# A decoder layer on one core: the late modulation sums move from VectorE to ScalarE products and accumulating DMAs

## The chip, the cores and the metric

The kernel runs on one core of one Trainium2 chip. Its time is the device time in microseconds (us) of that core for one execution of the whole program; three executions of the kernel before are known, and one execution was taken with a profile. TensorE is called PE here, its weight loads PEld, VectorE is DVE, ScalarE is ACT, GpSimd is POOL and SyncE is SP, as in the profile.

## The reference, cut to what matters

One layer, 512 tokens of width 1024, all in float32. A vector c gives six modulation vectors of width 1024 through one 1024 x 6144 matrix: shift, scale and gate of the attention half, and shift, scale and gate of the MLP half.

```python
c_act = silu(c)
mod = c_act @ w_ada + b_ada
sh1, sc1, g1, sh2, sc2, g2 = split(mod, 6)
h = rmsnorm(x, n0) * (1 + sc1) + sh1
y = token_mixer(h)                  # 8 MoBA heads, 8 sliding-window heads, output projection
x = x + g1 * rmsnorm(y, n1)
h = rmsnorm(x, n2) * (1 + sc2) + sh2
y = square(relu(h @ w1 + b1)) @ w2 + b2
x = x + g2 * rmsnorm(y, n3)
```

sh1 and sc1 are needed first and have code of their own, which the change leaves alone. The **later modulations** are g1, then sh2 and sc2 (in two halves), then g2: four units of work, each a 1024 x 1024 matrix times c_act.

## The kernel before

**The stages.** A first stage (up to about 70 us) loads x, normalises it and projects q and k for three pairs of heads. From there to about 240 us runs the attention: 64 blocks (16 heads of 4 query blocks of 128 tokens), and between their steps PE is given the rest of the input projection and, later, the output projection as filler. From about 260 us on, the MLP: 32 column groups up, 32 down, on PE almost without a gap. Each float32 matrix product is three fp32r matmuls (`mm3`, L95), for which weights and activations are split into a high and a low part: ACT makes the high part (L83), POOL or DVE the low part (L85).

**One attention block.** PE makes the scores; DVE adds the bias and takes the row extreme (L649); ACT takes the exponentials and their sum (L656); DVE takes the reciprocal (L662); POOL scales the row by it (L663, called the normalise below); PE transposes the result (L672); ACT and DVE split it (L686, L687). After the four blocks of a head PE makes its output, ACT and DVE bring it out of PSUM (L709, L710), and after each second head POOL splits it into `oth` and `otl` (L713, L715), which the output projection reads. Blocks are called w0_0 (head 0, block 0) to w15_3 below; the 64 normalises stand on POOL in this order.

**What sets the order.** PE's order is written by hand. For the other engines the library that builds the program orders each engine's instructions, within marks (`issue_after`) that put work behind the last bias on DVE and the last exponential on ACT (`anchor`, `behind`). Each engine runs its own list strictly in order, and an instruction that waits for a semaphore holds up all that stand behind it. SP issues nearly all loads, in order too.

**The late units.** `ada_wide(r, ...)` (L265) is a generator. For unit r it loads eight slices `adar{r}_0` to `adar{r}_7` of 128 x 1024 (512 KB each, four buffers, L274), and sums slice times c_act into `adaacc`, one half of 512 columns per step, by DVE (L282 for the first slice, L284 for the others): 16 steps. Then the sum over partitions is PE's: a product with ones (`adarow`, L299) for the gates, transposes (`adaps`, L242) and a DVE reduction for shift and scale. `side_at(k)` (L795) advances units 0, 1 and 2 by block number k. Unit 3 is advanced in the MLP, one step for each column group from the eighth on (L1042).

Of the kernel before, what the change touches and what calls it, by code (L numbers as in the profile page):

```python
# [23 lines left out]
AF = mybir.ActivationFunctionType  # L24
ALU = mybir.AluOpType
# [5 lines left out]
KC = DM // P  # L31
# [15 lines left out]
def layer_kernel(ctx, tc, x, c_col, ada_c, ada_r, bada_col, bada_row, gain_col, gain_row, w_in0, w_in1, w_in2,  # L47
                 w_out, w1, b1_col, w2, b2_row, rel, sinks, onehot, out):
    nc = tc.nc
# [149 lines left out]
    c_act = const.tile([P, KC], F32, name="c_act")  # L199
# [16 lines left out]
    def halves(t):  # L216
        return [t[:, 0:512], t[:, 512:1024]]
# [46 lines left out]

    def ada_wide(r, pool, then):  # L265

        acc = pool.tile([P, 1024], F32, tag="adaacc", name=f"adaacc{r}", bufs=1)
        raws = []

        def load():  # L270
            j = len(raws)
            if j < KC:
                raws.append(pool.tile([P, 1024], F32, tag="araw", name=f"adar{r}_{j}", bufs=4))
                nc.sync.dma_start(out=raws[j], in_=ada_r[r][:, j * 1024:(j + 1) * 1024])  # L274

        for _ in range(3):
            load()
        for j in range(KC):
            load()
            for a, w in zip(halves(acc), halves(raws[j])):  # L280
                if j == 0:
                    nc.vector.tensor_scalar_mul(a, w, c_act[:, j:j + 1])  # L282
                else:
                    nc.vector.scalar_tensor_tensor(a, w, c_act[:, j:j + 1], a, op0=ALU.mult, op1=ALU.add)  # L284
                yield
        then(acc)

    def gate_row(layer, g_bc, pool, tag):
# [116 lines left out]
    acc = next(g)  # L405
# [5 lines left out]
    for kc in range(KC):  # L411
# [3 lines left out]
        for k in range(18):  # L415
            if kc % 2 and nxt < KC:
                if k == 2:
                    grp = list(groups[(nxt + 2) // 2])
                    sums = ada_sums(0, grp, acc)
                    if nxt + 2 < KC:  # L420
                        g = acc0((nxt + 4) // 2)
                        acc = next(g)
# [11 lines left out]
            w, h = (w0[kc][0], hh) if k < 6 else (w0[kc][1], hh) if k < 12 else (w0[kc][0], hl)  # L434
# [37 lines left out]
    @contextmanager  # L472
    def behind():
        with ExitStack() as st:
            for ins in anchor.values():
                st.enter_context(tc.issue_after(ins))
            yield
# [308 lines left out]
    def side_steps():  # L786
        yield from ada_wide(0, wts, gate_row(0, g_bc, apool, "gt"))
        for r in range(2):
            kcs = list(range(4 * r, 4 * r + 4))
            yield from ada_wide(1 + r, wts, lambda acc: ada_cols(1, kcs, ada_sums(1, kcs, acc)))  # L790

    side = side_steps()
    sided = [1]

    def side_at(k):  # L795
        while sided[0] < 4 + min(k, 24) + max(0, min(k, 62) - 24) * 0.7 + max(0, k - 62):
            sided[0] += 1
            with behind() if k < len(blocks) else ExitStack():
                next(side, None)
# [25 lines left out]
    for k in range(len(blocks) + 8):  # L825
# [43 lines left out]
        if k < len(blocks) and blocks[k][2] == 2:  # L869
            strip_of(blocks[k][0] * 2 + blocks[k][1] + 1)  # L870
        side_at(k)
        if k < len(blocks):
            with behind():
# [158 lines left out]
    nc.sync.dma_start(out=b2_bc, in_=b2_row.to_broadcast([P, DM]))  # L1032
    g2_bc = mlp.tile([P, DM], F32, name="g2_bc")
    gate = ada_wide(3, wts, gate_row(1, g2_bc, res, "hf"))
    for f in range(3, NF):
        if f < 5:
            ws.make("both")
        w = ws.get(0 if f < 4 else 1)
# [20 lines left out]
    for f in range(NF - LAST):  # L1059
        w = ws.get()  # L1060
# [106 lines left out]
```

## Time and profile before

| | |
|---|---|
| median of three executions | 622.37 us (621.87 to 622.49) |
| the profiled execution | 623.07 us |
| its span, first to last instruction | 621.3 us, so 1.8 us lie outside it |
| PE busy | 580.3 us, 93% |
| DVE, ACT, POOL busy | 315.2, 279.2, 321.6 us |
| mean granted PE clock | 0.983 of full speed |

Busy times are sums of instructions, so a busy engine need not be the one that others wait for; what a stage waits for is read from the waits and from the order of time in that stage.

### The profile page before, as it was taken

Reading aid. Unit: us, or ns where it says so; the run is one execution under the profiler, and the core shown is the slowest. Engines: PE = TensorE matmul, PEld = TensorE weight load, DVE = VectorE, ACT = ScalarE, POOL = GpSimd, SP = SyncE. Lnnn points to the kernel's source line nnn. Section 1 sums busy time; section 2 is a strip of 40 time slices with the busy share of each in tenths; the row PEclk is TensorE's granted clock in tenths of the full one; section 3 lists DMA queues with packets and bytes.
Section 4 is the critical chain, followed back from the end, with each engine's and each line's share of the span. In section 5 each row is a group of like instructions: output and inputs, shape, how many; then the busy total and the mean of one; then the engine's idle time right before and its main releaser. Section 6 shows DMA issues by size and latency. Waiting matters only on the chain.

```text
span 621.3 us, 8137 instructions
## 1 busy us (share of the span) xinstructions
PE 580.3 (93%) x2829; PEld 482.0 (78%) x2829; DVE 315.2 (51%) x599; ACT 279.2 (45%) x532; POOL 321.6 (52%) x333
## 2 busy tenths in 40 slices
PE   2789989999897999999999999999999999999994
PEld 0477889887675888898888888788888888888883
DVE  4646679999998756535255555522401111111037
ACT  4624776578667545773233332233522333323122
POOL 1514234666898653636555555655544444446432
PEclk9969999999998999999999999999999999999998
DMA  8990569686466207734244432223232233333105
GB/s 308 419 383 1 189 129 260 128 170 224 140 185 207 84 1 270 236 106 149 89 136 136 146 125 99 80 93 101 71 112 89 100 103 102 102 101 116 56 17 186
DMA packets 29677, 89.31 MB, mean 144 GB/s; under 512 B 3427, under 2 KB 7587, under 8 KB 29636
## 3 DMA queue, kind: packets, MB, share of 16 engines
q1 hardware_dynamic: 28816, 86.52, 43.5%
q10 hardware_dynamic: 692, 2.23, 0.9%
q8 instruction: 22, 0.36, 0.3%
q14 instruction: 19, 0.16, 0.1%
q0 software_dynamic: 128, 0.05, 0.1%
HBM read 84.56 MB, written 4.22 MB: 143 GB/s over the span
## 4 chain that ended last, share of the span: by engine, by line
PE 55%; DVE 2%; ACT 2%; DMA 1%; issue 1%; POOL 0%; DVEq 0%; POOLq 0%; ACTq 0%; SPq 0%
PE u L97 9%; PE u L98 9%; PE u L96 9%; PE y L98 9%; PE y L97 9%; PE y L96 9%; DVE zg L1090 1%; ACT hf L379 1%; DMA x<-in_x 1%; ACT h2h L378 0%; DVE x L933 0%; DMA out_x<-zg 0%; ACT sq L208 0%; PE adarow L299 0%; POOL zg L1087 0%
## 5 line engine op out<-in xcount | busy, mean ns | idle before, releaser
L85 POOL TENSOR_TENSOR wlo<-raw,whi 128x512 fp32r<-128x512 f32 (+1 forms) x140 | 192.4, 1393 | 157.7 <-ACT whi L83 157.2
L83 ACT ACTIVATE whi<-raw 128x1024 fp32r<-128x1024 f32 (+5 forms) x87 | 80.7, 934 | 130.8 <-PE u L97 108.9
L97 PE MATMUL u<-h2l,whi 128*128 128x512 f32 (+1 forms) x280 | 104.2, 372 | 1.2 <-POOL h2l L380 1.1
L96 PE MATMUL u<-h2h,whi 128*128 128x512 f32 (+1 forms) x280 | 104.7, 374 | 0.0
L98 PE MATMUL u<-h2h,wlo 128*128 128x512 f32 (+1 forms) x280 | 103.8, 371 | 0.0
L97 PE MATMUL y<-wlo,ring_h2h 128*128 128x512 f32 x232 | 90.2, 389 | 0.0
L98 PE MATMUL y<-whi,ring_h2l 128*128 128x512 f32 x232 | 90.2, 389 | 0.0
L96 PE MATMUL y<-whi,ring_h2h 128*128 128x512 f32 x232 | 90.1, 389 | 0.0
L284 DVE SCALAR_TENSOR_TENSOR adaacc<-adar,c_act,adaacc 128x512 f32<-128x512 f32 x56 | 66.7, 1191 | 0.0
L97 PEld LDWEIGHTS u<-h2l,whi 128*128 128x128 f32 x280 | 52.7, 188 | 11.3 <-POOL h2l L380 1.7
L96 PEld LDWEIGHTS u<-h2h,whi 128*128 128x128 f32 x280 | 52.7, 188 | 9.2 <-ACT whi L83 0.2
L98 PEld LDWEIGHTS u<-h2h,wlo 128*128 128x128 f32 x280 | 52.7, 188 | 9.2
L663 POOL TENSOR_SCALAR w<-w,st 128x128 f32<-128x128 f32 (+2 forms) x64 | 38.2, 599 | 38.2 <-DVE st L662 32.8
L97 PEld LDWEIGHTS y<-wlo,ring_h2h 128*128 128x128 f32 x232 | 43.5, 188 | 9.1
L96 PEld LDWEIGHTS y<-whi,ring_h2h 128*128 128x128 f32 x232 | 43.5, 188 | 9.0
L98 PEld LDWEIGHTS y<-whi,ring_h2l 128*128 128x128 f32 x232 | 43.5, 188 | 9.0
L656 ACT ACTIVATE w<-w,st 128x128 f32<-128x128 f32 (+3 forms) x64 | 33.4, 522 | 28.2 <-DVE st L649 26.1
L85 POOL TENSOR_TENSOR w0lo<-w0raw,w0hi 128x384 fp32r<-128x384 f32 x16 | 17.2, 1095 | 29.3 <-ACT w0hi L83 29.3
L672 PE MATMUL p<-ident,w 128*128 128x128 f32 x136 | 25.9, 279 | 6.4 <-POOL w L663 5.9
L672 PEld LDWEIGHTS p<-ident,w 128*128 128x128 f32 x136 | 17.3, 142 | 13.4 <-POOL w L663 9.6
L686 ACT ACTIVATE pth<-p 128x384 fp32r<-128x384 f32 (+3 forms) x48 | 22.2, 466 | 10.1 <-PE p L672 9.6
L687 DVE TENSOR_TENSOR ptl<-p,pth 128x384 fp32r<-128x384 f32 (+3 forms) x48 | 25.0, 523 | 0.8 <-ACT pth L686 0.6
(222 smaller groups left out, 1093.9 us busy)
## 6 DMA issues: line engine op xcount, KB each, us to landing
raw<-in_w SPq DMA_DIRECT2D x63, 512.0 KB, 3.3
adar<-in_ada_r SPq DMA_DIRECT2D x32, 512.0 KB, 4.1
ada<-in_ada_c SPq DMA_DIRECT2D x16, 512.0 KB, 8.6
woraw<-in_w_out SPq DMA_DIRECT2D x8, 512.0 KB, 4.4
raw<-in_w_in SPq DMA_DIRECT2D x7, 512.0 KB, 6.7
w0raw<-in_w_in SPq DMA_DIRECT2D x8, 384.0 KB, 9.1
strip<-vec SPq DMA_DIRECT2D x24, 128.0 KB, 4.1
xn<-in_x SPq DMA_DIRECT2D x4, 512.0 KB, 10.0
```

The lines of the kernel that those rows point to most:

```text
L83: nc.scalar.activation(hi[:, a:b], src[:, a:b], AF.Copy)
L85: return eng.tensor_sub(lo[:, a:b], src[:, a:b], f32(hi[:, a:b])).ins
L96: nc.tensor.matmul(ps, lh, rh, start=start, stop=False, **kw)
L97: nc.tensor.matmul(ps, lh, rl, start=False, stop=False, **kw)
L98: nc.tensor.matmul(ps, ll, rh, start=False, stop=stop, **kw)
L284: nc.vector.scalar_tensor_tensor(a, w, c_act[:, j:j + 1], a, op0=ALU.mult, op1=ALU.add)
L379: nc.scalar.activation(hf[:, :n], tp, AF.Identity, bias=sh_col, scale=a_col)
L656: anchor["act"] = nc.scalar.activation(w[:, :m], w[:, :m], AF.Exp, bias=st[:, 0:1], scale=-1.0, accum_out=st[:, 1:2]).ins
L663: nc.gpsimd.tensor_scalar(w[:, :n], w[:, :n], st[:, 2:3], 1.0, op0=ALU.mult, op1=ALU.mult)
L672: nc.tensor.transpose(p_ps[:, (c0 + j) * P:(c0 + j + 1) * P], self.w[i][:, j * P:(j + 1) * P], ident)
L686: nc.scalar.activation(dst(self.pth), src, AF.Copy)
L687: nc.vector.tensor_sub(dst(self.ptl), src, f32(dst(self.pth)))
```

## The change

Each half slice is multiplied by ACT instead of DVE: slice 0 into `adaacc`, slices 1 to 7 in place in their own buffers. Slices 1 to 7 are then added onto `adaacc` by seven DMAs of 128 x 1024 with an add, issued from POOL's queue, both ends in SBUF. A unit now takes 19 steps instead of 16, and `side_at` advances faster.

```diff
@@ ada_wide @@
             for a, w in zip(halves(acc), halves(raws[j])):
-                if j == 0:
-                    nc.vector.tensor_scalar_mul(a, w, c_act[:, j:j + 1])
-                else:
-                    nc.vector.scalar_tensor_tensor(a, w, c_act[:, j:j + 1], a, op0=ALU.mult, op1=ALU.add)
+                nc.scalar.activation(w if j else a, w, AF.Copy, scale=c_act[:, j:j + 1])
                 yield
+                if j > 1 and a.offset == acc.offset:
+                    nc.gpsimd.dma_start(out=acc, in_=raws[j - 1], accum_op=ALU.add)
+        yield
+        nc.gpsimd.dma_start(out=acc, in_=raws[KC - 1], accum_op=ALU.add)
+        yield
+        yield
         then(acc)
@@ side_at @@
-        while sided[0] < 4 + min(k, 24) + max(0, min(k, 62) - 24) * 0.7 + max(0, k - 62):
+        while sided[0] < 4 + min(k, 24) * 1.2 + max(0, min(k, 62) - 24) * 0.8 + max(0, k - 62):
```

In the program that results, lines behind L284 stand four lines further down (the normalise is L667, `oth` L717, `otl` L719, the small power for the root of a norm stays L213); DVE loses 64 instructions, ACT gains 64 and POOL's queue 28 DMAs. They are called accumulates below, 0_1 to 3_7 by unit and slice.

POOL in the attention's first heads, before (w is a block's row of weights, the number behind it the head, then the block):

```order
L663 TENSOR_SCALAR w1_0_813<-w1_0_813,st1_0_864 128x128 [waits DVE_49]
L663 TENSOR_SCALAR w1_1_859<-w1_1_859,st1_1_892 128x256 [waits DVE_49,PE_49]
L663 TENSOR_SCALAR w1_2_887<-w1_2_887,st1_2_929 128x384 [waits DVE_49,PE_49]
L663 TENSOR_SCALAR w1_3_920<-w1_3_920,st1_3_955 128x512 [waits DVE_49,PE_49]
L663 TENSOR_SCALAR w2_0_950<-w2_0_950,st2_0_981 128x128 [waits DVE_49,PE_49]
```

The same place now (a DMASW semaphore counts the completion of a DMA from POOL's queue, eight of them in turn, so DMASW6 here is the accumulate of slice 3, DMASW7 that of slice 4, DMASW0 that of slice 5):

```order
L667 TENSOR_SCALAR w1_0_816<-w1_0_816,st1_0_869 128x128 [waits DVE_49]
L285 DMA adaacc0_674<-adar0_4_708 128x1024 [waits DMAHW7_49,DMASW6_49,Activation_49]
L667 TENSOR_SCALAR w1_1_864<-w1_1_864,st1_1_896 128x256 [waits DVE_49,PE_49]
L667 TENSOR_SCALAR w1_2_891<-w1_2_891,st1_2_935 128x384 [waits DVE_49,PE_49]
L285 DMA adaacc0_674<-adar0_5_738 128x1024 [waits DMAHW0_49,DMASW7_49,DMASW0_49]
L667 TENSOR_SCALAR w1_3_926<-w1_3_926,st1_3_961 128x512 [waits DVE_49,PE_49]
L667 TENSOR_SCALAR w2_0_956<-w2_0_956,st2_0_988 128x128 [waits DVE_49,PE_49]
```

Accumulates now stand between the normalises, and each waits for the one before it.

POOL at the end of the attention, before, from the split of head pair 6 (`of6`) to the first root of a norm:

```order
L715 TENSOR_TENSOR otl1_1953<-of6_2476,oth1_1952 128x256 [waits Pool_49]
L715 TENSOR_TENSOR otl1_1953<-of6_2476,oth1_1952 128x256
L713 TENSOR_SCALAR oth1_1952<-of7_2626 128x512 [waits DVE_49]
L715 TENSOR_TENSOR otl1_1953<-of7_2626,oth1_1952 128x256 [waits Pool_49]
L715 TENSOR_TENSOR otl1_1953<-of7_2626,oth1_1952 128x256
L213 TENSOR_TENSOR s2_0_2685<-s2_0_2685,mhalf_155 128x1 [waits DVE_49]
```

And now:

```order
L719 TENSOR_TENSOR otl1_1968<-of6_2497,oth1_1967 128x256 [waits Pool_49]
L719 TENSOR_TENSOR otl1_1968<-of6_2497,oth1_1967 128x256
L285 DMA adaacc3_3373<-adar3_4_3452 128x1024 [waits DMAHW5_49,DMASW3_49]
L285 DMA adaacc3_3373<-adar3_5_3524 128x1024 [waits DMAHW6_49,DMASW4_49]
L285 DMA adaacc3_3373<-adar3_6_3597 128x1024 [waits DMAHW7_49,DMASW5_49,Activation_49]
L717 TENSOR_SCALAR oth1_1967<-of7_2647 128x512 [waits DVE_49]
L719 TENSOR_TENSOR otl1_1968<-of7_2647,oth1_1967 128x256 [waits Pool_49]
L719 TENSOR_TENSOR otl1_1968<-of7_2647,oth1_1967 128x256
L287 DMA adaacc3_3373<-adar3_7_3670 128x1024 [waits DMAHW0_49,DMASW6_49,Activation_49]
L213 TENSOR_TENSOR s2_0_2706<-s2_0_2706,mhalf_155 128x1 [waits DVE_49]
```

Unit 3, which had its DVE steps inside the MLP, now has its ACT products and its accumulates in the last blocks of the attention: only DVE work was held back by the MLP's mark, and none of unit 3 is DVE's any more. Three accumulates in a row stand ahead of the last head pair's split.

## Rows read from the trace of the kernel before

**Rows 1.** The page, part 1: busy us (share of span) xinstructions.

```profile
PE 580.3 (93%) x2829; PEld 482.0 (78%) x2829; DVE 315.2 (51%) x599; ACT 279.2 (45%) x532; POOL 321.6 (52%) x333
```

**Rows 2.** Busy time by stretch of the attention; the first line names the columns.

```profile
core 0: us, PE busy (x) PEld busy (x) DVE busy (x) ACT busy (x) POOL busy (x), PEclk, DMA share, GB/s
75.00:150.00 75.00, 72.28 (x433) 64.36 (x431) 69.59 (x172) 53.34 (x136) 38.42 (x45) 1.00 0.76 190
150.00:210.00 60.00, 51.42 (x281) 41.77 (x282) 54.67 (x151) 40.69 (x103) 49.24 (x77) 0.94 0.58 174
210.00:240.00 30.00, 30.00 (x169) 25.56 (x169) 17.61 (x46) 16.94 (x41) 15.37 (x29) 1.00 0.20 76
```

**Rows 3.** Waits, whole run: engine line <- releaser: us in total, times, longest us.

```profile
POOL w L663 <- DVE st L662: 32.8, 19, 10.6
...
ACT w L656 <- DVE st L649: 26.1, 26, 2.3
...
PE p L672 <- POOL w L663: 5.9, 8, 1.6
```

**Rows 4.** The instructions on adaacc: count, duration ns min/median/max, first and last start us.

```profile
L284 DVE SCALAR_TENSOR_TENSOR adaacc<-adar,c_act,adaacc x56: 724/1059/1881, 54.0 to 395.5; 128x512 f32<-128x512 f32 x56
```

**Rows 5.** Groups by shape: xcount | busy us, mean ns | idle before.

```profile
L319 ACT ACTIVATE acc<-ada,c_act 128x512 f32<-128x512 f32 x6 | 4.0, 710 | 0.0
...
L178 POOL DMA_DIRECT2D bada_c<-in_bada_col x1 | 0.8, 764 | 0.8 <-POOLq L1159 0.8
...
L184 POOL DMA_DIRECT2D sink_t<-in_sinks x1 | 0.5, 534 | 0.0
```

**Rows 6.** DMA issues: tensors, queue, count, KB each, median us to landing.

```profile
adar<-in_ada_r SPq DMA_DIRECT2D x32, 512.0 KB, 4.1
...
x_d<-x ACTq DMA_DIRECT2D x4, 512.0 KB, 2.8
...
c_sb<-in_c_col SPq DMA_DIRECT2D x1, 4.0 KB, 2.3
bada_c<-in_bada_col POOLq DMA_DIRECT2D x1, 16.0 KB, 4.5
```

**Rows 7.** The loads of adar by themselves.

```profile
DMA to landing us min/median/max: 3.5/4.1/10.3
```

**Rows 8.** POOL in order of time: start us, us, instruction, [idle before].

```profile
83.84 0.78 POOL L663 TENSOR_SCALAR w<-w,st 128x128 f32<-128x128 f32 x1 [10.56 <-DVE st L662]
...
110.23 0.97 POOL L663 TENSOR_SCALAR w<-w,st 128x512 f32<-128x512 f32 x1 [2.23 <-DVE st L662]
...
123.96 1.63 POOL L663 TENSOR_SCALAR w<-w,st 128x512 f32<-128x512 f32 x2 [0.62 <-DVE st L662]
...
149.66 0.48 POOL L663 TENSOR_SCALAR w<-w,st 128x256 f32<-128x256 f32 x1 [0.79 <-DVE st L662]
...
170.36 0.47 POOL L663 TENSOR_SCALAR w<-w,st 128x256 f32<-128x256 f32 x1
...
201.04 0.47 POOL L663 TENSOR_SCALAR w<-w,st 128x256 f32<-128x256 f32 x1
...
213.81 0.62 POOL L713 TENSOR_SCALAR oth<-of 128x512 fp32r<-128x512 f32 x1
...
226.24 1.43 POOL L715 TENSOR_TENSOR otl<-of,oth 128x256 fp32r<-128x256 f32 x2
...
234.44 0.62 POOL L713 TENSOR_SCALAR oth<-of 128x512 fp32r<-128x512 f32 x1 [6.76 <-DVE of L710]
```

**Rows 9.** PE in order of time at three places.

```profile
112.13 1.45 PE L299 MATMUL adarow<-adaacc,ones 128*128 128x512 f32 x3
...
151.36 0.55 PE L672 MATMUL p<-ident,w 128*128 128x128 f32 x3 [0.49 <-POOL w L663]
...
235.63 0.39 PE L96 MATMUL y<-wo2h,oth 128*128 128x512 f32 x1
```

## The prediction

> **What bounds the kernel now.** I read the page's busy times first. PE works 580.3 of 621.3 us [rows 1], so over the whole run PE is the bound, and a change elsewhere pays or costs only where it lets PE idle. The table by stretch shows where that can be [rows 2]. From 75 to 150 us PE is busy 72.28 of 75, from 150 to 210 us 51.42 of 60, from 210 to 240 us all of it; in the MLP behind that it has no gaps. So 2.7 and 8.6 us of idle PE lie in the attention, and in the second stretch the granted clock is 0.94, which costs 0.06 x 51.42 = 3.1 us more. These 14.4 us are all that relief of another engine could give. In the same stretches DVE is busy 69.59 of 75 and 54.67 of 60, the fullest but PE.
>
> The waits come next [rows 3]. POOL's normalise waits for DVE's reciprocal (32.8 us in all), ACT's exponential for DVE's row extreme (26.1), and PE's transposes for POOL's normalise (5.9 in 8 waits): the chain of a block is DVE, ACT, DVE, POOL, PE, and it has little slack. Last I read POOL and PE in order of time, for the places where the accumulates are put [rows 8, 9].
>
> **What the change removes.** 56 DVE multiply-adds of about 1.06 us [rows 4], and 8 first products. Unit 3's lie in the MLP, where PE is full: nothing to gain. Of units 0 to 2, 42 x 1.06 = 45 us leave DVE between 54 and 210 us. The gain is between 0 and the 14.4 us above. Most of PE's idle time lies in 150 to 210 us, where POOL too is busy 49.24 of 60 [rows 2], so that DVE is only a part of its cause; I take 4.
>
> The multiply-adds take 724 to 1881 ns for one and the same shape [rows 4]. The Trainium skill, "SBUF — State Buffer", section "Who interferes with whom", says that a DVE instruction with two inputs in SBUF contends with GpSimd's reads. The spread agrees, and by it some of POOL's own time could shrink as well; the 14.4 us stay the ceiling.
>
> **What it adds on ACT.** 64 products of 128x512. The nearest row is ACT's biasing of the same shape, 0.71 us [rows 5]: 45 us, 34 of them for units 0 to 2. ACT is busy 53.34 + 40.69 = 94 of 135 us between 75 and 210 [rows 2], so they fit in its idle time, but each can delay an exponential by up to 0.71. Unit 3's products are new in 210 to 240 us, where ACT is busy 16.94 of 30: about eleven fall there, 8 us, and the products wait for loads that wait for accumulates, ahead of the last heads' exponentials. I take 2 us, from 0 to 8.
>
> **What it adds on POOL.** 28 issues at 0.53 to 0.76 us [rows 5], say 0.55. POOL is tight only from 150 to 210 us: seven issues there, 3.9 us, of which I take half, 2.
>
> The larger cost is the wait. Each accumulate waits for the landing of the one before, and POOL keeps its order, so whatever stands behind a waiting accumulate is held: normalises, splits of weights, `oth` and `otl`, the roots of the norms. And behind the normalises PE waits. Let t be the time from an accumulate's issue to its landing. No accumulate and no SBUF to SBUF transfer is in the trace. The nearest rows: 512 KB stored out of SBUF land in 2.8 us from ACT's queue; small loads land in 2.3 us from SP's queue and 4.5 from POOL's [rows 6], so POOL's queue costs some 2.2 more. An estimate from both: t = 2.8 + 2.2 = 5.0. The low end is 2.8. The high end is 8, where the add's second stream and other traffic count in full: the 512 KB loads need 3.5 to 10.3 us, median 4.1 [rows 7].
>
> The Trainium skill, "DMA: Bandwidth & Descriptors", section "Anatomy of one DMA — SWDGE (gpsimd) path", gives about 2.0 us plus bytes over 436 GB/s for a DMA from this queue, 3.2 us for 512 KB. By it the ledger below would come to 2.3 instead of 13.9 us, and the kernel would be about unchanged or faster. The row of POOL's own queue, 4.5 us for 16 KB, is longer than the page has for thirty times the bytes.
>
> **The ledger, unit by unit** (ends are start plus duration [rows 8, 9]; the places are from the changed order, two pieces of which are shown above):
> - Unit 0. 0_2 stands behind w0_0, free at 84.62; 0_7 behind w2_3, free at 111.20. 26.6 us for five landings of 5: nothing is held on POOL. But 0_7 lands at 116.2, and PE's `adarow`, at 112.13, needs it: 4.1 us.
> - Unit 1. 1_1 stands behind w3_3 (about 124.93), 1_7 behind w6_1 (150.14). 25.2 us for six landings, 30: 4.8 us. PE's next transposes wait for POOL already (0.49 ahead of 151.36), so it has no slack.
> - Unit 2. 2_1 behind w8_2 (170.83), 2_7 behind w12_1 (201.51): 30.7 us for 30, nothing.
> - Unit 3. 3_1 stands behind `oth` of head pair 6 and three normalises at the earliest at 214.43, and 3_4 to 3_6 in a row ahead of the last `oth`, which starts at 234.44 before, at once after its input. 3_6 can't be issued before 214.43 + 25 = 239.4; with its issue and the `oth` of 0.62 that is 240.6, where PE's first `y` matmul on it stands at 235.63: 5.0 us. `otl` of the pair before ends at 227.67, so with t at 4 the bound comes from there: 227.67 + 8 + 1.17 is 236.8, 1.2 us. 3_7 stands before the first root of a norm, where PE still has other `y` work.
>
> Together 13.9 us at t = 5; 2.3 at 3.2; 4.3 at 4; 35 at 6; 46 at 6.5. In this ledger the step from a hidden to a visible chain lies between t = 4 and t = 5.
>
> After such stalls PE's clock can fall, as it has in 150 to 210 us already (0.94 there against 1.00 ahead and behind [rows 2]); one more such stretch is 3 us, I take 2. The slower issue of loads at the start costs nothing: products of 0.71 stand in for multiply-adds of 1.06. The later place of the last `adarow` in the MLP costs nothing either, as `g2` is read at the end only.
>
> Sum: 13.9 + 2 (ACT) + 2 (POOL issues) + 2 (clock) - 4 (DVE) = 15.9. The profiled execution took 623.07 us, 0.7 above the median of 622.37, so 639.0 on the profile's scale and 638.3 on the median's; I say 639.
>
> **Rivals.**
> - *Landings over 6 us.* From 75 to 150 us the DMA engines are 0.76 busy at 190 GB/s [rows 2], 14.3 MB; twelve accumulates add 6.3 MB, which at the same efficiency makes 1.1, more than there is. The accumulates then queue behind loads and each other. Against it: part of those loads is early and can slide to later stretches (0.58, 0.20). At t = 6.5: 46 + 2 - 1 more, 670.
> - *ACT becomes the bound, landings hidden.* 94 + 34 = 128 of 135 us, and its waits for DVE [rows 3] come on top as far as they stay: 128 + 26 is 19 us too much, and half of the waits should go with DVE's relief: about 9 us, 632. Against it: the exponentials' waits shrink with the very DVE work that moves.
> - *Faster.* Accumulates land in 3.5 us or less; then no chain is seen, only `adarow`'s 2.3 us, and DVE's relief gives PE its 8.6 idle us between 150 and 210 back. 623.07 + 2.3 - 8.6 is 616.8. It decides at t of about 3.5 to 4. For it: the store of 512 KB in 2.8; against it: POOL's queue in [rows 6].
> - *No net change.* t about 4: 4.3 lost, 4 given back, 622 to 623.
>
> **How the numbers follow.** The chain with t from 4.3 to 6: 0.50, 639, its own range 627 to 658. Landings over 6: 0.18, 670. ACT the bound: 0.12, 632. Faster: 0.14, 616. No net change: 0.06. The range of 618 to 672 leaves out half of the faster case and half of the slowest, 0.16. 0.2% of the time, 1.2 us, is about what a measurement of this kernel can tell from none; beyond it faster has 0.14, slower 0.80, within it 0.06.
>
> **What would show it.** In the changed profile: accumulates from POOL's queue at about 5 us to landing; a new wait of POOL for its own DMA queue of tens of us in all; PE's waits for normalises up from 5.9 to over 10; `adarow` of unit 0 and the last `oth` each some 4 to 5 us late; DVE's busy time lower by about 60 and ACT's higher by 45. The prediction is wrong if landings are near 3 (then faster), if POOL does not wait behind them, or if the time is lost on ACT instead: exponentials waiting behind products, with the normalises on time.

## The result, and the profile after

The changed kernel takes 686.98 us (median of four, 686.86 to 689.32), the kernel before 622.12 beside it: a ratio of 1.1052, 95% interval 1.1027 to 1.1077. It is slower by 64.9 us. The forecast was slower, at 639 us and at most 672.

Part 1 of the changed kernel's page:

```profile
PE 598.7 (87%) x2829; PEld 494.5 (72%) x2829; DVE 254.0 (37%) x535; ACT 316.3 (46%) x596; POOL 329.8 (48%) x361
```

Against [rows 1], DVE lost 61 us of work and ACT gained 37, about as forecast (60 and 45). None of it shows as a gain in the time. The table by stretch says where the time went (the columns are those of [rows 2]):

```profile
75.00:150.00 75.00, 60.46 (x347) 54.06 (x345) 41.96 (x114) 51.32 (x122) 25.92 (x38) 0.91 0.74 171
150.00:210.00 60.00, 42.82 (x218) 35.66 (x217) 27.44 (x91) 41.12 (x95) 34.88 (x52) 0.83 0.75 181
210.00:240.00 30.00, 21.50 (x108) 16.61 (x106) 15.87 (x50) 21.35 (x50) 17.18 (x33) 0.86 0.80 208
```

PE, busy 153.7 of these 165 us before, is busy 124.8 now. And nobody else is busy in its place: DVE, ACT and POOL all did less in the stretch from 75 to 150 us than before. All engines wait. The groups of DMA issues show for whom (queue, count, KB each, median us to landing), and the answer on L285 gives min, median and max for the accumulates but each unit's last:

```profile
adaacc<-adar POOLq DMA_DIRECT2D x28, 512.0 KB, 6.4
adar<-in_ada_r SPq DMA_DIRECT2D x32, 512.0 KB, 3.8
```

```profile
DMA to landing us min/median/max: 4.5/6.5/9.8
```

POOL in order of time, in unit 0 and, from 165.98 us on, in unit 1:

```profile
84.45 0.90 POOL L285 DMA_DIRECT2D adaacc<-adar  x1 [0.75 <-ACT adar L282]
87.22 0.47 POOL L667 TENSOR_SCALAR w<-w,st 128x256 f32<-128x256 f32 x1 [1.87 <-DVE st L666]
89.44 0.88 POOL L285 DMA_DIRECT2D adaacc<-adar  x1 [1.75 <-ACT pth L690]
...
108.46 0.87 POOL L285 DMA_DIRECT2D adaacc<-adar  x1 [6.47 <-issue]
109.09 1.32 POOL L667 TENSOR_SCALAR w<-w,st 128x512 f32<-128x512 f32 x2
115.46 0.90 POOL L285 DMA_DIRECT2D adaacc<-adar  x1 [5.05 <-DMA adaacc<-adar]
...
165.98 0.89 POOL L285 DMA_DIRECT2D adaacc<-adar  x1 [5.14 <-ACT pth L690]
166.60 1.60 POOL L85 TENSOR_TENSOR wlo<-raw,whi 128x512 fp32r<-128x512 f32 x1
167.89 0.77 POOL L667 TENSOR_SCALAR w<-w,st 128x256 f32<-128x256 f32 x1
...
186.21 0.89 POOL L287 DMA_DIRECT2D adaacc<-adar  x1 [4.13 <-DMA adaacc<-adar]
```

The reader is to see two things. POOL stands 4 to 6.5 us ahead of several accumulates (6.47, 5.05, 5.14 and 4.13 above), and what it does behind one comes in a burst. And the releaser named is not always the one: an accumulate waits for several semaphores, and here the profile names an "issue" or ACT. The times of the landings settle it. In the trace, accumulates landed at 107.94, 115.09, 165.25 and 185.86 us, and the next was issued 0.52, 0.37, 0.73 and 0.35 us later. So it is, within 0.92 us, for 23 of the 24 that follow another of their own unit; only the second of unit 0 stood behind something else.

The marks of the ledger, PE at the head of `adarow`, at the transposes behind unit 1 and at the last head pair's first `y`, against 112.13, 151.36 and 235.63 in [rows 9]:

```profile
128.61 2.90 PE L303 MATMUL adarow<-adaacc,ones 128*128 128x512 f32 x3 [7.72 <-DMA adaacc<-adar]
...
189.01 0.90 PE L676 MATMUL p<-ident,w 128*128 128x128 f32 x3 [7.45 <-POOL w L667]
...
294.01 0.50 PE L96 MATMUL y<-wo2h,oth 128*128 128x512 f32 x1 [2.10 <-POOL oth L717]
```

They are 16.5, 37.7 and 58.4 us late. One more step is lost behind them. The last accumulate, 3_7, waits for the landing of 3_6 (302.26), and the first root of a norm stands behind it on POOL:

```profile
302.84 0.89 POOL L287 DMA_DIRECT2D adaacc<-adar  x1 [7.37 <-issue]
303.46 1.42 POOL L213 TENSOR_TENSOR s<-s,mhalf 128x1 f32<-128x1 f32 x2
```

DVE had the root's input ready at 297.60 us. PE then waits for what follows from the root; from 290 to 345 us its waits show

```profile
PE tp L375 <- DVE z L945: 4.6, 2, 4.0
```

From the first store of a token tile on, 64.3 us later than before, nothing more is lost: the last `y` of the MLP is 63.9 us later. The delay grows unit by unit, here by the start of the normalise of a block:

| block | 0 | 16 | 32 | 48 | 63 |
|---|---|---|---|---|---|
| before, us | 83.8 | 125.2 | 165.8 | 199.3 | 224.2 |
| after, us | 83.3 | 142.6 | 201.3 | 243.3 | 275.4 |
| later by | -0.5 | 17.4 | 35.5 | 44.0 | 51.2 |

### The profile page after: what moved, and what is told of

The parts are those of the page before. It is cut to its first block, busy times and chain, and to the rows that moved or that the text cites. A ratio compares the mean times of both kernels' runs of the same rounds, so it can differ in the third digit from the quotient of the medians.

```text
span 685.1 us, 8202 instructions
## 1 busy us (share of the span) xinstructions
PE 598.7 (87%) x2829; PEld 494.5 (72%) x2829; DVE 254.0 (37%) x535; ACT 316.3 (46%) x596; POOL 329.8 (48%) x361
## 3 DMA queue, kind: packets, MB, share of 16 engines
q0 software_dynamic: 4160, 14.73, 10.9%
## 4 chain that ended last, share of the span: by engine, by line
PE 52%; DVE 1%; issue 1%; ACT 0%; POOL 0%; DMA 0%; DVEq 0%; POOLq 0%; ACTq 0%
PE u L97 9%; PE u L98 8%; PE u L96 8%; PE y L97 8%; PE y L98 8%; PE y L96 8%; DVE zg L1094 1%; PE tp L375 1%; DMA out_x<-zg 0%; PE adarow L303 0%; POOL zg L1091 0%; ACT sq L208 0%; POOL s L213 0%; ACT sqz L208 0%; DVEq L1167 0%
## 5 line engine op out<-in xcount | busy, mean ns | idle before, releaser
L667 POOL TENSOR_SCALAR w<-w,st 128x128 f32<-128x128 f32 (+2 forms) x64 | 40.6, 679 | 25.4 <-DVE st L666 25.1
L285 POOL DMA_DIRECT2D adaacc<-adar x24 | 21.4, 893 | 61.6 <-DMA adaacc<-adar 18.6
L282 ACT ACTIVATE adar<-adar,c_act 128x512 f32<-128x512 f32 x56 | 38.8, 713 | 18.9 <-DMA adar<-in_ada_r 18.9
L676 PE MATMUL p<-ident,w 128*128 128x128 f32 x136 | 28.3, 301 | 16.4 <-POOL w L667 16.4
L676 PEld LDWEIGHTS p<-ident,w 128*128 128x128 f32 x136 | 18.9, 154 | 24.3 <-POOL w L667 19.9
L653 DVE CUSTOM_DVE_ANT_0 w<-s,strip 128x128 f32<-128x128 f32 (+3 forms) x32 | 15.6, 489 | 45.1 <-PE s L646 31.1
```

What stands on the lines that cost most here:

```text
L282: nc.scalar.activation(w if j else a, w, AF.Copy, scale=c_act[:, j:j + 1])
L285: nc.gpsimd.dma_start(out=acc, in_=raws[j - 1], accum_op=ALU.add)
L653: anchor["dve"] = nc.vector.tensor_tensor_reduce(w[:, :n], self.s[i][:, :n], self.strip[:, 512 - n:], scale=1.0, scalar=init, op0=ALU.add, ...
L667: nc.gpsimd.tensor_scalar(w[:, :n], w[:, :n], st[:, 2:3], 1.0, op0=ALU.mult, op1=ALU.mult)
L676: nc.tensor.transpose(p_ps[:, (c0 + j) * P:(c0 + j + 1) * P], self.w[i][:, j * P:(j + 1) * P], ident)
```

## The experiments

Theory A is the prediction's own: POOL waits out a chain of accumulates in order. The rivals: B, ACT's products; C, the traffic of the accumulates on the DMA engines; D, unit 3 at the end of the attention. Times of before are those measured beside each.

**e1_products_only: the products without the accumulates.**

```diff
-                if j > 1 and a.offset == acc.offset:
-                    nc.gpsimd.dma_start(out=acc, in_=raws[j - 1], accum_op=ALU.add)
-        nc.gpsimd.dma_start(out=acc, in_=raws[KC - 1], accum_op=ALU.add)
```

> The changed kernel without its 28 accumulates: ACT's 64 products and the steps stay, the seven later slices of each unit are left out of the sums. Theory A, the chain of accumulates that POOL waits out in order: all of the loss is gone and DVE's relief shows, 613 to 623 us. Theory B, ACT's products and their waits for loads: most of the loss stays, over 650. Theory C, the accumulates load the DMA engines and so slow the other loads: as A. Theory D, unit 3 at the end of the attention: about 640, since its products are still there.

622.46 us against 621.78, ratio 1.001 (0.9985 to 1.0036). All of the loss is gone with the accumulates. So B is out as its cause, and so is D as far as it means unit 3's products; its accumulates are e6's question. But nothing is gained either.

**e2_accumulates_only: the accumulates almost without the products.**

```diff
-                nc.scalar.activation(w if j else a, w, AF.Copy, scale=c_act[:, j:j + 1])
+                n = 1 if j else 512
+                nc.scalar.activation((w if j else a)[:, 0:n], w[:, 0:n], AF.Copy, scale=c_act[:, j:j + 1])
```

> The changed kernel with its 28 accumulates in their places, but of each later product only one column of 512 is multiplied, so that ACT's 0.71 us become a short instruction. Theory A (chain on POOL): 677 to 690 us, since the waits are those of the changed kernel. Theory B (ACT's products): under 645. C as A; D between, about 670.

683.45 us, ratio 1.0988 (1.0964 to 1.1013). The loss is there without ACT's work.

**e4_plain_copy: copies for the adds** (`accum_op` left out of the three lines).

> Each accumulate is a plain copy of the same 512 KB onto the same tile from the same queue (the sum is left out), same order, same waits. It measures what the add costs in t. If t stays at 6.4 us the add is free and the time stays at 680 to 690. If the add's second stream is the reason for t over my 5.0, copies land in about 5 and, by the ledger at a period of 5.5 us (22.6 us instead of 54.8 at 6.9), the time is 645 to 655. Theory B expects no change in either case.

653.94 us, ratio 1.0515 (1.0488 to 1.0542). POOL's queue (packets, MB, share of 16 engines) on the page of the changed kernel, then on that with copies, and the copies' landings:

```profile
q0 software_dynamic: 4160, 14.73, 10.9%
```

```profile
q0 software_dynamic: 4160, 14.73, 5.6%
```

```profile
DMA to landing us min/median/max: 2.9/4.9/9.5
```

10.9% of 685.1 us, over 28, is 2.67 us of every engine for one accumulate; 5.6% of 650.6 is 1.30 us for a copy of the same bytes (both with the queue's few small transfers). The add doubles the work of the engines, and alone on them an accumulate lands in 4.4 us (the least of the 28), a copy in 2.9. The Trainium skill, "DMA: Bandwidth & Descriptors", section "Anatomy of one DMA — SWDGE (gpsimd) path", gives 2.0 us plus the bytes over 436 GB/s for a DMA from this queue, by which 512 KB would take an estimated 3.2 us: about right for the copy alone (2.9), short for the accumulate (4.4), and half of what it took in this traffic (6.4). With landings shorter by a fifth, half of the loss was gone, in the way of the ledger.

**e6_unit3_in_mlp: unit 3 back in the MLP.**

```diff
-        nc.scalar.activation(rsq(f), ps, AF.Relu, bias=b1_c[:, f:f + 1])
+        relu2.act = nc.scalar.activation(rsq(f), ps, AF.Relu, bias=b1_c[:, f:f + 1])
...
-            with tc.issue_after(last.ins):
+            with tc.issue_after(last.ins), tc.issue_after(relu2.act.ins), tc.issue_after(ws.last_lo):
```

> As the changed kernel, but ACT's products and POOL's accumulates of unit 3 are held back to the column groups of the MLP, where DVE's sums stood before. Theory A: unit 3's share of the ledger comes back, 14.5 by its formula at a period of 6.9 and 17 as read after the change, 668 to 674 us; in the MLP accumulates stand some 11 us apart and cost nothing. Theory D (unit 3 is the cause): under 640.

674.37 us, ratio 1.0829 (1.0797 to 1.0862): 12.6 us come back, a little less than unit 3's share, and D is out as the main cause. (Unit 3's products move as well, so not all of the 12.6 us need be its accumulates'.) In the MLP, seven accumulates cost nothing: from the first store of a token tile to the MLP's last `y` it is 370.2 us, as before the change. They land in

```profile
DMA to landing us min/median/max: 6.4/6.6/6.9
```

longer than the 4.4 us alone, though the engines are less full there (DMA share 0.63 from 380 to 460 us). The order of time has the reason: for the last six of the seven, a load of weights is issued 0.08 to 0.09 us behind the accumulate, as here.

```profile
406.34 0.86 POOL L285 DMA_DIRECT2D adaacc<-adar  x1
406.43 0.33 SPq L111 DMA_DIRECT2D raw<-in_w  x1
```

That load is served first all the same. It lands at 410.77 us, the accumulate at 413.23, and the accumulate's first packet starts 3.3 us after its issue, where that of one alone (84.45 above) starts after 1.5.

**e9_small_loads: is it the load that stands ahead?**

```diff
-                nc.sync.dma_start(out=raws[j], in_=ada_r[r][:, j * 1024:(j + 1) * 1024])
+                nc.sync.dma_start(out=raws[j][:, 0:128], in_=ada_r[r][:, j * 1024:j * 1024 + 128])
...
-                nc.scalar.activation(w if j else a, w, AF.Copy, scale=c_act[:, j:j + 1])
+                nc.scalar.activation(w if j else a, ones[:, 0:1].to_broadcast([P, 512]), AF.Copy, scale=c_act[:, j:j + 1])
```

> The changed kernel, but each load of a slice brings 128 columns of 1024, and the products read a constant tile of the same shape, so that ACT's work, the accumulates and their order stay nearly as they are (the sums are not those of the slices). In the changed kernel the load that an accumulate's landing sets free stands in the DMA engines ahead of the next accumulate. If that is what lifts t from 4.45 (alone) to 6.4, t falls to about 5 and the time to 645 to 660, as with the plain copies. If t stays over 6, the time stays at 675 to 690 and the cause of the long landings is another.

671.11 us, ratio 1.0791 (1.0766 to 1.0815), over my range.

```profile
DMA to landing us min/median/max: 4.4/4.8/11.1
```

The median fell from 6.4 to 4.8 as expected: in the changed kernel a landing frees a buffer, SP issues the next load into it within 0.1 us (0.46 in one case), and the accumulate that POOL issues 0.3 to 0.9 us after the landing finds that load ahead of it. But I had taken the median for the sum. The mean fell only from 6.72 to 5.95, as the loads of weights and of the attention's bias strips still came in its way (up to 11.1 us). By the mean the time fits, see below.

**e7_products_unit3_mlp and e13_neither: what DVE's relief is worth.** e7 is e1 with e6's edit; e13 is e7 with e2's edit.

> As e1_products_only (no accumulates, later slices left out of the sums), and ACT's products of unit 3 are held back to the MLP. In e1 the normalises were up to 8 us ahead of the kernel before at block 44 and only 2 ahead at the end, and unit 3's products stand in between. If they are what gives the gain back: 614 to 618 us. If the gain is lost for another reason (ACT as full as DVE was, or the clock): 619 to 623, and then ACT's products can bring nothing here, whatever is done about the adds.

> As e7_products_unit3_mlp (617.7 us), but of each later product only one of 512 columns is multiplied: the sums cost DVE nothing and ACT next to nothing. What DVE's relief is worth at most: if ACT's products cost what e7 didn't gain of the 14.4 us of idle PE and slow clock, 608 to 614 us; if DVE was never the cause of most of it, 615 to 618.

617.73 us, ratio 0.9933 (0.9910 to 0.9956), and 609.11 us, ratio 0.9812 (0.9769 to 0.9856). The attention by stretch, e7, then e13:

```profile
75.00:150.00 75.00, 74.50 (x446) 66.34 (x445) 52.75 (x158) 70.34 (x169) 35.21 (x49) 1.00 0.74 184
150.00:210.00 60.00, 53.53 (x306) 44.55 (x305) 42.72 (x136) 52.38 (x124) 42.14 (x83) 0.97 0.50 162
```

```profile
75.00:150.00 75.00, 75.00 (x456) 67.62 (x455) 55.24 (x165) 63.88 (x178) 37.11 (x54) 1.00 0.74 185
150.00:210.00 60.00, 56.97 (x341) 48.10 (x340) 46.57 (x150) 49.04 (x129) 48.24 (x90) 1.00 0.48 154
```

Without DVE's sums and without ACT's products PE is full from 75 to 150 us and the clock stays at 1.00: 12 us, near the ceiling of 14.4. With the products (ACT at 70.34 of 75 us) some 4 are left, and with unit 3's products in the last heads too, as in e1, none. So ACT's products cost about 8 us of their own, and in these placements the change could have brought 4 at most, had the adds been free.

**e11_even_rate and e8_tree: the same bytes with less waiting.** Both have e6's edit. e11 spreads the steps evenly, 0.9 for each block; e8 takes 0.95, as shown here, with 21 steps for a unit instead of 19, and adds in a tree.

```diff
-        while sided[0] < 4 + min(k, 24) * 1.2 + max(0, min(k, 62) - 24) * 0.8 + max(0, k - 62):
+        while sided[0] < 4 + min(k, 62) * 0.95 + max(0, k - 62):
...
+        adds = iter([(None, 1), (2, 3), (4, 5), (None, 2), (None, 4), (6, 7), (None, 6)])
+
+        def add():
+            to, of = next(adds)
+            nc.gpsimd.dma_start(out=acc if to is None else raws[to], in_=raws[of], accum_op=ALU.add)
...
+                if (j, h) in ((2, 0), (4, 0), (6, 0), (6, 1), (7, 1)):
+                    add()
```

> As e6_unit3_in_mlp (674 us), accumulates in one chain, but the steps are spread evenly, 0.9 for each block. Theory A: 21 accumulates at 6.9 us are 145 us, and the blocks offer some 150: POOL waits where they still bunch, 640 to 662 us, over e8 by 15 or more. Theory C: as e8.

> The sum as it should be, by a tree: 1 onto the sum, 3 onto 2, 5 onto 4, 2 and 4 onto the sum, 7 onto 6, 6 onto the sum, so that most accumulates do not need the one just ahead; even rate of 0.95 steps for each block; unit 3 held back to the MLP. Theory A: the serial wait is mostly gone, POOL's waits for accumulates fall under 15 us, and what is left is the issues (21 of 0.6 us) and adds still on the path: 622 to 640 us. Theory C (it is the DMA traffic and not the waiting): 655 to 675, as the bytes are the same.

e11: 677.47 us, ratio 1.0890 (1.0870 to 1.0910), a miss. Its landings were longer (mean 7.12), the chain too long for the room in spite of the even rate. PE waited 25.9 us for normalises, and for the ends of the chains 12.1 us more (`adaps`). e8: 648.95 us, ratio 1.0441 (1.0411 to 1.0472), between the two ranges. With the same 28 accumulates of the same bytes and landings nearly as long (mean 6.60), most of them no longer the successor of the one just ahead, 28 us of e11's loss are gone. The places and the rate differ a little too, so the 28 us are not the tree's to the last one. But they are not C's, since the bytes are the same; the traffic makes the landings long. What it costs besides in the 27 us that are left, no run separates. And a tree is not enough: POOL still waits for accumulates into slices, 17.5 us, and PE for normalises, 13.5 us.

**e12_eighth and e14_eighth_free: short accumulates.** e12 adds 128 of 1024 columns (`acc[:, 0:128]`, `raws[j - 1][:, 0:128]`); e14 leaves these columns out of the products as well.

> The changed kernel with accumulates of 128 columns instead of 1024 (the rest of each later slice is left out of the sums), in one chain and nearly the same places. Alone such an accumulate should take about 2.2 us (4.45 less seven eighths of the 2.65 us that the engines worked on it), and the load ahead of it stays, so t is about 3.7 to 4.2 and the period 4.3 to 4.8. Theory A: the ledger gives 4 to 11 us at that period, DVE's relief takes 0 to 4 off: 620 to 633 us. If the 28 stops of POOL cost by themselves, whatever their length: over 645.

> As e12_eighth (646 us, 13 us above its ledger), but the products leave out the 128 columns that the accumulates read, so that an accumulate waits for its load and for the accumulate before it, and no longer for ACT's product (some accumulates then stand a few places earlier on POOL). In e12 POOL stood ahead of accumulates until some work of ACT or DVE was done for 28 of its 40 us, and until an accumulate landed for 6. If the wait for the product behind ACT's other work is the excess: 626 to 636 us. If the stops cost by themselves: 643 to 648.

646.31 us, ratio 1.0413 (1.0371 to 1.0456), and 639.50 us, ratio 1.0285 (1.0257 to 1.0313). Both missed. The landings in e12:

```profile
DMA to landing us min/median/max: 2.3/3.6/8.9
```

2.3 us alone, as worked out (2.2); but up to 8.9 in traffic, mean 4.24. In e14's expectation I read e12's waits by the releaser that the profile names, mostly ACT, and that was wrong as shown above: in e12, too, 20 of the 24 were issued 0.3 to 1 us after a landing. What e14 gave back, 6.8 us, goes with a shorter period (4.54 us for 5.05), but its accumulates also stand earlier on POOL (0_7 is issued at 92.94 us, in e12 at 111.83).

## Why the prediction was right in its mechanism and wrong in its size

**The step that failed is t, the landing, taken as 5.0 us** (2.8 for a store, 2.2 for POOL's queue [rows 6]), and with it the period of the chain, for which I used t and left out the pause between a landing and the next issue. The mean landing was 6.72 us and the mean pause 0.52 (without the one of 24 us in unit 0), a period of 7.24. The landing alone takes the ledger from 13.9 to 51.1 us, the pause to 62.5. A third term was put at nothing without a row: 3_7, ahead of the first root of a norm, cost PE 4.6 us.

The ledger's sum held. With each run's own mean landing and pause put into the same formulas, places and marks of [rows 8, 9]:

| run | mean landing | pause | ledger: unit 0 + 1 + 2 + 3 | measured loss |
|---|---|---|---|---|
| changed kernel | 6.72 | 0.52 | 15.4 + 18.2 + 12.7 + 16.2 = 62.5 | 64.9 |
| e2, hardly any products | 6.82 | 0.50 | 64.3 | 61.7 |
| e9, small loads | 5.95 | 0.70 | 48.9 | 49.4 |
| e6, unit 3 in the MLP (units 0 to 2) | 6.91 | 0.51 | 16.5 + 19.3 + 13.8 = 49.6 | 52.6 |
| e4, plain copies | 5.25 | 0.70 | 32.6 | 32.2 |
| e12, an eighth | 4.24 | 0.81 | 13.6 | 25.3 |
| e14, an eighth, freed | 4.14 | 0.40 | 7.9 | 18.2 |

(In e12 the pause is long because a few accumulates had to wait for other things.) The first five agree within 3 us over a range of 32 to 65. Part of that is luck, as the parts agree less than the sum. By PE's marks of the changed kernel, unit 0 cost 16.5 us (ledger 15.4), unit 1 21.2 (18.2), units 2 and 3 together up to the first `y` 20.7 (28.9), and 3_7 another 4.6 (nothing). Nor is it a forecast: each run's landings had to be measured in that run.

At short landings the ledger is too low by 10 to 12 us. The row of e14 is not a fair test, since its accumulates left the ledger's places. For e12 two causes are argued, and no run shows either by itself. The ledger takes a mean, and lets a quick landing make up for a slow one; POOL can't, as an accumulate has its place and is not issued ahead of it, so that chains of uneven landings cost earlier than the prediction's sharp step between t = 4 and 5. And the 28 issues take POOL's time whatever they move; the prediction has 2 us for them, and no run keeps the issues and takes all of the waits away.

**Why t was too short.** Two things that no row of before could show as a price: the add doubles the engines' time (1.30 to 2.67 us, e4), and the chain brings its own traffic, since most landings free a buffer whose load then stands ahead of the next accumulate (e9: median 6.4 to 4.8). Alone, an accumulate takes 4.4 us, less than my 5.0. The row that was nearest to the truth was that of the loads, 3.5 to 10.3 us [rows 7], which I had used for the high end alone.

**The rivals.** "Landings over 6 us", 0.18 and 670 us, was the right case, and accumulates did queue behind loads. But its reason, engines asked for 1.1 of their time, is not needed for that: the share was 0.74, 0.75 and 0.80 in the three stretches, and in the MLP of e6, at 0.63, landings still took 6.4 to 6.9 us, there behind a single load. It gave 670 for t = 6.5 where the time came at 687, again by the missing pause, the mean of 6.72 and 3_7. "ACT becomes the bound" is not what happened, but its price was near: e13 against e7 puts ACT's products at some 8 us. (Its 9 us does not follow from its own words: 19 less half of the 26 us of waits is 6.) "Faster" and "no net change" needed landings that did not come.

**The small terms.** DVE's relief is 12 us with nothing in its place (e13), 4 beside ACT's products of units 0 to 2 (e7), none with unit 3's products in the last heads (e1). I had 4 less 2 for ACT: of the right size together. In the changed kernel it can't be seen, because behind a wait of POOL every engine has time. The clock fell to 0.91, 0.83 and 0.86 in the three stretches, more than the one stretch that I had counted at 2 us; in e13, without stalls, it is 1.00 in all of them. PE's busy time rose from 580.3 to 598.7 us for the same 2829 matmuls. How much of these 18.4 us lies hidden in the waits, and how much adds to the loss, no run separates.

The prediction's remark that POOL's own time could shrink is borne out where DVE's sums are gone. The same normalise, from 75 to 240 us, before and in e13:

```profile
L663 POOL TENSOR_SCALAR w<-w,st 128x512 f32<-128x512 f32 x8 | 7.5, 940 | 8.1 <-DVE st L662 8.0
```

```profile
L665 POOL TENSOR_SCALAR w<-w,st 128x512 f32<-128x512 f32 x8 | 5.9, 736 | 9.4 <-DVE st L664 8.8 <-PE p L674 0.6
```

It takes 736 ns for 940, in e7 710. In the changed kernel, beside the issues of the accumulates, it takes 886, so little of it shows there.

**What stays open:** the last 12 us at short landings, the price of the slower clock, and whether accumulates placed so far apart that each has landed before POOL comes to the next would leave the 4 us of e7. None of these runs that computes the whole sums is faster than the kernel before.

## What to carry to other kernels

Work that is handed to a DMA is cheap only when nobody stands behind its completion: in an in-order queue that also serves the critical path, each link of a chain of dependent DMAs costs its landing, plus the pause to the next issue, less the work that was due in between anyway. Price the landing in the traffic that the change itself brings: which transfer does each landing set free, and does it stand ahead of the next link? And before moving work off a busy engine, let it vanish and see what that is worth; here it was 12 us, of which the products cost 8 on the engine that took them.

## What was not expected of the hardware

- A DMA that adds occupies the DMA engines twice as long as one that copies the same 512 KB: 2.67 against 1.30 us of each engine, 4.4 against 2.9 us to landing when alone.
- An accumulate lets a load go ahead that is issued with it: beside one load of 512 KB that was issued 0.08 us after it, it landed in 6.4 to 6.9 us in the MLP of e6, against 4.4 alone.
- POOL is busy 0.89 us with the issue of one accumulate, but its next instruction starts 0.6 us after it (108.46 to 109.09 above), so that the 28 issues cost less than their busy time.
- Eight times fewer bytes shorten the least landing only from 4.4 to 2.3 us, and the median from 6.4 to 3.6.
